# Three groups of token tiles in place of four, on a transformer block with a gathered expert layer

## The chip, the cores and the metric

The kernel runs on one core of a Trainium2 chip. The metric is device time in microseconds. Three runs of the kernel before gave 3733.66, 3748.12 and 3753.72; the median is 3748.12.

## What is computed

One trunk layer over 1024 latent tokens (8 tiles of 128) and 256 context tokens, width 1024, all in fp32. Cut to what matters:

```python
z = modulate(h_lat, sh_a, sc_a) @ w_in            # context tokens alike
q, k, v = mla_project(...)                         # 8 heads, 128 + 64 wide, low rank
att = softmax(q @ k.T * scale) @ v                 # keys: context and latent, 1280
s5 = bidirectional state-space layer               # second branch
merged = sigmoid(gate_mla) * att + sigmoid(gate_s5) * glu(s5)
h = layer_norm(ALPHA * h + g_a * (merged @ w_out), ln1)
# PEER: 8 heads, top 16 of 128 x 128 experts each
s = einsum(xb @ wq, keys); sv, si = top_k(s, 16)   # two halves
top_s, experts = top_k(sums of both halves, 16)    # 128 experts a token
act = gelu(einsum('thkd,td->thk', u_tab[experts], xb))
f = einsum('thk,thkd->td', softmax(top_s) * act, v_tab[experts])
out = layer_norm(ALPHA * h + g_f * f, ln2)
```

## The kernel before, in words

The 8 latent tiles are numbered 0 to 7. Up to about 480 us the input projection, the state-space layer, keys and values are made for all tiles and parked in HBM. Then the tiles go through in groups (`GROUPS`), here (0), (1, 2), (3, 4, 5), (6, 7). `front` does one group: `attention` (for each head the keys are loaded and split into a high and a low part once, then used for every tile of the group; a tile with a head is called a tile-head below), `gates` (weights of the gates and the GLU, loaded and split once a group), `close` (output projection and two norms), and the preparation of the next group's queries (`prepare`). It returns `route`, the expert selection of the group, which isn't run at once: the next group's `attention` takes `TSTEP` steps of it after each head. A step is one routing head.

The expert layer has three forms. Tiles 2 to 5 (`DENSE`) go through all 16384 experts as matmuls at the end (`dense`); after their routing, `spread` writes their weights as a matrix beside the next group's gates. Tiles 6 and 7 (`VEC`) gather rows of both tables beside the dense part. Tiles 0 and 1 gather too, in the front: for each of 128 experts a token, POOL issues an indirect DMA of a row of `peer_u` per token (L1271), DVE multiplies and sums it (L1275); then it gathers the row of `peer_v` (L1351) and PE adds it into two accumulators in PSUM by four matmuls with a diagonal (L1356). Six row buffers are shared by all gathers. The gathers of `peer_v` of a tile need all its 128 products; those of tile 0 lie between the gathers of tile 1.

The order on each engine is made by a scheduler from the written order, priorities (`PRIO`) and its own estimate of times; each engine then runs its instructions strictly in that order. `HOLDS` adds to this: a product of L1275 is placed behind a named instruction. For tile 0 the products from the 36th on stand behind the preparation of group 2 (mark p2), for tile 1 from the 100th on behind that of group 3 (p3). The dense part needs the two PSUM accumulators of tile 1's sum, so its second half of each step comes behind that sum.

Of the kernel before, what the change touches and what calls it, by code (L numbers as in the profile page):

```python
# [8 lines left out]
F32 = mybir.dt.float32  # L9
# [21 lines left out]
WBUFS = 4  # L31
NRES = 4
NEI = 3
RB = 6
SCB = (3, 3, 2, 2)
SC2 = (1, 1, 1, 1)
CAB = (1, 1, 1, 1)
OHB = (1, 1, 1, 1)
QHB = (2, 2, 1, 1)
H2B = 1  # L40
HMB = 2
GROUPS = ((0,), (1, 2), (3, 4, 5), (6, 7))
DENSE = (2, 3, 4, 5)
VEC = (6, 7)
TSTEP = (2, 2, 2)
TPRE = (0, 0, 0)
CHUNK = 32
GTP = 2
GTB = 2
VCUT = 2  # L50
STB = (1, 1, 1, 1)
SPLIT = (False, False, True, False)
SUBS = (((0,),), ((0, 1),), ((0, 1, 2),), ((0, 1),))
CENG = "VVVV"
WQB = 2
GSTEP = 10
# [2 lines left out]
RPRIO = 2500  # L59
MSTEP = 2  # L60
XLOAD = 4
GSIDE = ('right', 'right', 'right', None)
CSIDE = ("right", "right", "right", None)
SETTLE = 2
PREP = (0, 9, 9, None)
GSPLIT = (True, True, True, True)
GWB = 2
EBS = (2, 2, 2, 4)
EBANK = "S"
PRIO = (0, 1500, 1500, 3000, 2000)  # L70
PACE = 8
RAT = 3
TWAIT = 2
S0 = 36
P0 = 128
S1 = 100
P1 = 128
M0 = "p2"
M1 = "p3"
HOLDS = {0: [(M0, S0)] + [("r1.%d" % h, S0 + P0 * (h + 1)) for h in range(8)],  # L80
         1: [(M1, S1)] + [("r2.%d" % h, S1 + P1 * (h + 1)) for h in range(8)],
         6: [("t3", 0)]}
KENG = ((), (), (), ())
GENG = ((), (), (), ())
EVERY = (1, 2, 1)
LEAD = (0, 32, 0)

# [2 lines left out]
def block_kernel(ctx: ExitStack, tc: tile.TileContext, a: dict, out: bass.AP):  # L90
# [3 lines left out]
    def pool(name, bufs=1, side=None, space=None):  # L94
        kw = {"name": name, "bufs": bufs}
        if side:
            kw["side"] = side
        if space is not None:
            kw["space"] = space
        return tc.alloc_tile_pool(**kw)  # L100
# [24 lines left out]
    hm_d = tc.dram_tile([NT, 128, 8 * 128], F32, name="hm_d")  # L125
# [74 lines left out]
    W = pool("W")  # L200
# [3 lines left out]
    def wload(src, shape):  # L204

        t = W.tile([128, 2048], F32, tag="w", bufs=WBUFS, name="w")
        n = 1
        for d in shape[1:]:
            n *= d
        names = "abcd"[:len(shape) - 1]  # L210
        dims = {names[i]: shape[i + 1] for i in range(len(names))}
        flat = " ".join(names)
        v = t[:, 0:n] if len(shape) == 2 else t[:, 0:n].rearrange(f"p ({flat}) -> p {flat}", **dims)
        last[0] = SY.dma_start(v, src)
        return v
# [227 lines left out]
    for i in range(5):  # L443
        w = 1 << i
# [7 lines left out]
    t1, t2 = c32("sq0"), c32("sq1")  # L452
# [293 lines left out]
    def prepare_loads(gi):  # L746

        grp = GROUPS[gi]
        P = pool("P%d" % gi) if gi else None
        SY.dma_start(R["q"][2], a["rope_feat"][:, :, 128 * grp[0]:128 * grp[0] + 128 * len(grp)])  # L750
        if not gi:
            w = wload(a["w_cq"][0:2].rearrange("j p a b -> p j a b"), [128, 2, 8, 128])
            w = [w[:, 0], w[:, 1], wload(a["w_cq"][2], [128, 8, 128])]
            return P, w, [wload(hm_d[grp[0] + 2].rearrange("p (a b) -> p a b", a=8), [128, 8, 128])]
        w = P.tile([128, 3, 8, 128], F32, tag="wcq", name="wcq")
        hms = [P.tile([128, 8, 128], F32, tag="hm%d" % i, name="hm") for i in range(len(grp))]
        for i, l in enumerate(grp):
            SY.dma_start(hms[i], hm_d[l + 2].rearrange("p (a b) -> p a b", a=8))
            if i == 0:
                SY.dma_start(w, a["w_cq"].rearrange("j p a b -> p j a b"))  # L760
        return P, [w[:, j] for j in range(3)], hms

    def prepare(gi, P, w, hms):

        cqT = R["q"][1]
        for i, hmT in enumerate(hms):
            pa = bank("mm", "pa")
            for j in range(3):
                for k in range(8):
                    PE.matmul(pa[:, j * 128:(j + 1) * 128], hmT[:, k, :], w[j][:, k, :], start=(k == 0), stop=(k == 7))  # L770
            nq = (P or W).tile([128, 384 if P else 2048], F32, tag="nq" if P else "w", bufs=2 if P else WBUFS, name="nq")[:, 0:384]
            ss = cols.tile([128, 1], F32, tag="ss", name="ss")
            S.activation(nq, pa[:, 0:384], func=AF.Square, accum_out=ss)
            rs = rstd_of(ss, EPS, 1.0 / 384)
            marks["p%d" % gi] = V.tensor_scalar(nq, pa[:, 0:384], rs, None, op0=MUL)
            pt = bank("tp", "ptc", (128, 4, 128))
            for j in range(3):
                PE.transpose(pt[:, j, :], nq[:, j * 128:(j + 1) * 128], eye)
            for j in range(3):
                S.activation(cqT[:, j, i * 128:(i + 1) * 128], pt[:, j, :], func=AF.Copy, scale=qng[:, j:j + 1])  # L780
        if P:
            P.release()

    def open_queries(gi):
        Q = pool("Q%d" % gi, side="right")
# [201 lines left out]
    def route(gi, grp, H, h2T):  # L987
# [57 lines left out]
        places = []  # L1045
        for sub in SUBS[gi]:
            for h in range(8):
# [8 lines left out]
                for z in range(2):  # L1056
# [14 lines left out]
                    pz = bank("mm", "pz")  # L1071
                    sc_ = B.tile([128, ntok], F32, tag="sc", bufs=SCB[gi], name="sc")
                    for i in sub:
# [521 lines left out]
```

## Time and profile before

| | |
|---|---|
| median of 3 runs | 3748.12 us |
| profiled execution | 3734.93 us |
| its span, first to last instruction | 3733.2 us |
| mean granted TensorE clock | 0.948 |
| busy share PE, DVE, ACT, POOL | 90%, 79%, 35%, 40% |

Shares are of the whole span. PE's matmuls are pipelined and their ends are modelled, so a busy PE is not PE at its peak. Line numbers are those of the kernel before.

### The profile page before, as it was taken

How to read it: one execution, taken by the hardware profiler on the slowest of the kernel's cores; microseconds unless marked ns; L12 is line 12 of the kernel's file. 1: busy time of each engine (PE TensorE's matmuls, PEld its weight loads, DVE VectorE, ACT ScalarE, POOL GpSimd, SP SyncE). 2: the span in 40 equal slices, each digit the busy share in tenths (PEclk: the TensorE clock that was granted, in tenths of full speed). 3: DMA queues.
4: the chain of work that ended last, by engine and by line, in shares of the span. 5: the costliest groups of instructions: out<-in, count | busy, mean ns of one | idle time of the engine just before them, and what ended most of it. 6: DMA issues, size and time to landing. Idle time of an engine off the chain costs nothing.

```text
span 3733.2 us, 54383 instructions
## 1 busy us (share of the span) xinstructions
PE 3359.1 (90%) x20022; PEld 2733.2 (73%) x20022; DVE 2956.9 (79%) x6996; ACT 1297.7 (35%) x2329; POOL 1491.9 (40%) x1254
## 2 busy tenths in 40 slices
PE   5978888979779989869999969999999999999997
PEld 3745577869667668757769758878888888888885
DVE  7358755685798879689968877888888888889895
ACT  2223353443123444033345443333333333333332
POOL 5045400041355564443442100265655555546540
PEclk7978999989889989979999979999999999999998
DMA  8742276476698898987898763599999999989992
GB/s 280 236 85 73 89 264 228 156 301 244 224 347 309 316 338 324 362 308 289 295 355 314 296 232 124 181 368 340 330 342 333 339 335 340 340 325 355 340 328 79
DMA packets 348714, 1032.46 MB, mean 277 GB/s; under 512 B 46592, under 2 KB 142080, under 8 KB 322592
## 3 DMA queue, kind: packets, MB, share of 16 engines
q0 software_dynamic: 147456, 536.94, 39.3%
q1 hardware_dynamic: 164032, 462.20, 34.9%
q10 hardware_dynamic: 36960, 29.86, 2.5%
q8 instruction: 157, 2.57, 0.3%
q14 instruction: 109, 0.89, 0.1%
HBM read 961.27 MB, written 67.62 MB: 276 GB/s over the span
## 4 chain that ended last, share of the span: by engine, by line
PE 56%; DVE 9%; issue 8%; DMA 7%; ACT 2%; POOL 2%; DVEq 0%; POOLq 0%; ACTq 0%
PE turn L1235 6%; PE turn L1237 6%; PE turn L1236 6%; PE fd L1196 5%; PE fd L1197 5%; PE fd L1198 5%; DMA vb<-in_peer_v,eiT 4%; DVE ub L1275 3%; PE po L954 2%; PE acc L1356 2%; PE pqr L1066 2%; PE pe L1153 2%; DMA ub<-in_peer_u,ei 2%; POOL ub L1271 1%; PE po L809 1%
## 5 line engine op out<-in xcount | busy, mean ns | idle before, releaser
L1271 POOL DMA_INDIRECT ub<-in_peer_u,ei x512 | 654.9, 1279 | 1212.9 <-DVE ub L1275 438.4
L1275 DVE SCALAR_TENSOR_TENSOR ub<-ub,h 128x1024 f32<-128x1024 f32 x512 | 616.3, 1217 | 59.5 <-DMA ub<-in_peer_u,ei 59.2
L1318 POOL DMA_INDIRECT vb<-in_peer_v,ei x256 | 361.8, 1413 | 268.2 <-DVE f L1321 205.5
L1351 POOL DMA_INDIRECT vb<-in_peer_v,eiT x256 | 288.7, 1128 | 400.4 <-PE acc L1356 324.8
L1235 PE MATMUL turn<-hh,u 128*128 128x512 f32 x1024 | 401.7, 392 | 0.0
L1236 PE MATMUL turn<-hh,u 128*128 128x512 f32 x1024 | 400.2, 391 | 0.0
L1237 PE MATMUL turn<-hl,u 128*128 128x512 f32 x1024 | 400.1, 391 | 0.0
L1197 PE MATMUL fd<-v,kpe_l 128*128 128x512 f32 x887 | 351.7, 397 | 1.5 <-DVE kpe_l L234 1.5
L1198 PE MATMUL fd<-v,kpe_h 128*128 128x512 f32 x887 | 349.6, 394 | 0.0
L1196 PE MATMUL fd<-v,kpe_h 128*128 128x512 f32 x887 | 339.3, 396 | 0.0
L1321 DVE SCALAR_TENSOR_TENSOR f<-vb,zz,f 128x1024 f32<-128x1024 f32 x254 | 325.4, 1281 | 2.8 <-DMA vb<-in_peer_v,ei 0.2
L1239 ACT ACTIVATE act<-turn 128x512 f32<-128x512 f32 x128 | 76.6, 598 | 578.7 <-PE turn L1237 578.6
L233 ACT CAST v<-w 128x1024 fp32r<-128x1024 f32 x128 | 134.7, 1053 | 269.1 <-PE fd L1197 269.0
L1235 PEld LDWEIGHTS turn<-hh,u 128*128 128x128 f32 x1024 | 192.3, 188 | 42.0
L1237 PEld LDWEIGHTS turn<-hl,u 128*128 128x128 f32 x1024 | 192.3, 188 | 41.9
L1236 PEld LDWEIGHTS turn<-hh,u 128*128 128x128 f32 x1024 | 192.3, 188 | 40.4
L1356 PE MATMUL acc<-vb,diag 128*32 128x256 f32 x2048 | 159.8, 397 | 51.1 <-DMA vb<-in_peer_v,eiT 51.0
L1198 PEld LDWEIGHTS fd<-v,kpe_h 128*128 128x128 f32 x887 | 166.8, 188 | 41.4
L1196 PEld LDWEIGHTS fd<-v,kpe_h 128*128 128x128 f32 x887 | 166.9, 188 | 40.8
L1197 PEld LDWEIGHTS fd<-v,kpe_l 128*128 128x128 f32 x887 | 166.9, 188 | 40.5 <-DVE kpe_l L234 1.8
L234 DVE TENSOR_TENSOR v<-w,v 128x1024 fp32r<-128x1024 f32 x128 | 156.2, 1221 | 33.4 <-ACT v L233 32.8
L1241 DVE TENSOR_TENSOR act<-act,gt 128x512 f32<-128x512 f32 x128 | 88.6, 692 | 118.2 <-ACT act L1239 117.9
(421 smaller groups left out, 8143.2 us busy)
## 6 DMA issues: line engine op xcount, KB each, us to landing
w<-in_peer_uT SPq DMA_DIRECT2D x64, 1024.0 KB
w<-in_peer_v SPq DMA_DIRECT2D x64, 1024.0 KB
w<-in_peer_wq SPq DMA_DIRECT2D x32, 1024.0 KB
gT_d<-stage SPq DMA_DIRECT2D x16, 2048.0 KB
gt<-gT_d SPq DMA_DIRECT2D x32, 1024.0 KB
vh<-v_d SPq DMA_DIRECT2D x32, 640.0 KB
w<-k_d SPq DMA_DIRECT2D x32, 640.0 KB
w<-in_w_mod_b SPq DMA_DIRECT2D x16, 1024.0 KB
```

Source lines behind the costliest of these rows:

```text
L1196: PE.matmul(o, ah[:, ts], vh[:, cs], start=first, stop=False)
L1197: PE.matmul(o, al[:, ts], vh[:, cs], start=False, stop=False)
L1198: return PE.matmul(o, ah[:, ts], vl[:, cs], start=False, stop=final)
L1235: PE.matmul(turn, uh[:, k, :], hh[:, k, :], start=(k == 0), stop=False)
L1236: PE.matmul(turn, ul[:, k, :], hh[:, k, :], start=False, stop=False)
L1237: PE.matmul(turn, uh[:, k, :], hl[:, k, :], start=False, stop=(k == 7))
L1271: GP.indirect_dma_start(out=ub, out_offset=None, in_=a["peer_u"], in_offset=bass.IndirectOffsetOnAxis(ap=ei[:, s:s + 1], axis=0))
L1275: V.scalar_tensor_tensor(ub, ub, 1.0, h2, op0=MUL, op1=MUL, accum_out=dots[:, s:s + 1])
L1318: GP.indirect_dma_start(out=vb, out_offset=None, in_=a["peer_v"], in_offset=bass.IndirectOffsetOnAxis(ap=ei[:, s:s + 1], axis=0))
L1321: V.scalar_tensor_tensor(f, vb, z[:, s:s + 1], f, op0=MUL, op1=ADD)
L1351: GP.indirect_dma_start(out=vb, out_offset=None, in_=a["peer_v"], in_offset=bass.IndirectOffsetOnAxis(ap=eiT[:, t:t + 1], axis=0))
L1356: PE.matmul(acc[d // 2][o:o + 32, 256 * (d % 2):256 * (d % 2) + 256], dg[:, q, jj, :], vb[:, d * 256:(d + 1) * 256], start=False, stop=Fal ...
```

## The change

The groups become (0, 1, 2), (3, 4, 5), (6, 7). Routing of the first group runs as two sub-groups: eight steps for tile 0, two idle steps, then eight steps for tiles 1 and 2 and again two idle ones, three steps after each head. The marks p2, p3 and the holds of tiles 0 and 1 go; that of tile 6 stays, under the new group number. Several per-group buffer counts change: the routing of the first group has two score buffers and one query buffer, where before groups (0) and (1, 2) had three and two. Preparation of the second group comes behind the closing of all tiles of the first; before, that of (1, 2) came behind the closing norm of tile 0.

```diff
-SCB = (3, 3, 2, 2)
+SCB = (2, 2, 2)
-QHB = (2, 2, 1, 1)
+QHB = (1, 1, 1)
-GROUPS = ((0,), (1, 2), (3, 4, 5), (6, 7))
+GROUPS = ((0, 1, 2), (3, 4, 5), (6, 7))
-TSTEP = (2, 2, 2)
+TSTEP = (3, 2)
-SPLIT = (False, False, True, False)
-SUBS = (((0,),), ((0, 1),), ((0, 1, 2),), ((0, 1),))
+SPLIT = (False, True, False)
+SUBS = (((0,), (1, 2)), ((0, 1, 2),), ((0, 1),))
-PREP = (0, 9, 9, None)
+PREP = (9, 9, None)
-EBS = (2, 2, 2, 4)
+EBS = (2, 2, 4)
-PRIO = (0, 1500, 1500, 3000, 2000)
+PRIO = (0, 1500, 3000, 2000)
-RAT = 3
+RAT = 2
-HOLDS = {0: [(M0, S0)] + [("r1.%d" % h, S0 + P0 * (h + 1)) for h in range(8)],
-         1: [(M1, S1)] + [("r2.%d" % h, S1 + P1 * (h + 1)) for h in range(8)],
-         6: [("t3", 0)]}
+HOLDS = {6: [("t2", 0)]}
...
     def prepare_loads(gi):
         grp = GROUPS[gi]
-        P = pool("P%d" % gi) if gi else None
+        P = pool("P%d" % gi)
...
-            return P, w, [wload(hm_d[grp[0] + 2].rearrange("p (a b) -> p a b", a=8), [128, 8, 128])]
+            two = wload(hm_d[2:4].rearrange("l p (a b) -> p l a b", a=8), [128, 2, 8, 128])
+            return P, w, [two[:, 0], two[:, 1], wload(hm_d[4].rearrange("p (a b) -> p a b", a=8), [128, 8, 128])]
```

The gathers stand in the same order on POOL in both kernels. Three places of the new order matter. Lines of the changed kernel are 8 lower than before in these places.

On PE the first group's attention begins with the preparation (pa, ptc) and the query projection (pq) of its tiles. Before:

```order
L770 MATMUL pa<-w 128x128 x24
L778 MATMUL ptc<-eye,nq 128x128 x3
L821 MATMUL pq<-cqT,w 128x128 x12
L858 MATMUL pS<-kh,qnh 128x512 x2
L858 MATMUL pS<-kh,qnh 128x256
```

and now:

```order
L763 MATMUL pa<-w 128x128 x48
L771 MATMUL ptc<-eye,nq 128x128 x3
L763 MATMUL pa<-w 128x128 x24
L771 MATMUL ptc<-eye,nq 128x128 x6
L813 MATMUL pq<-cqT,w 128x384 x12
L850 MATMUL pS<-kh,qnh 128x512 x2
L850 MATMUL pS<-kh,qnh 128x256
```

Three tiles are prepared before the first score, and the projection's matmuls are as many, but three times as wide. No routing matmul stands before the end of this attention.

On DVE the ids of tile 0 (ei) are followed by its first product with a gathered row (ub). Before, this lies in the attention of tiles 1 and 2, whose maxima and sums are mx, mb and smx:

```order
L1034 SCALAR_TENSOR_TENSOR ef<-pi 128x64
L863 TENSOR_REDUCE mx<-pS 128x1
L234 TENSOR_TENSOR kl<-w,kh 128x512
L1103 CAST ei<-ef 128x128
...
L800 RECIPROCAL smx<-smx 128x1
L1275 SCALAR_TENSOR_TENSOR ub,dots<-ub,h_17879 128x1024
L863 TENSOR_REDUCE mx<-pS 128x1 x2
```

Now it lies in the attention of tiles 3, 4 and 5, behind its twelfth tile-head:

```order
L1026 SCALAR_TENSOR_TENSOR ef<-pi 128x64
L1095 CAST ei<-ef 128x128
L1101 CAST eiT<-ptE 128x128
L1267 SCALAR_TENSOR_TENSOR ub,dots<-ub,h_17468 128x1024
L986 MAX V_8531<-sc 128x8 x2
L1267 SCALAR_TENSOR_TENSOR ub,dots<-ub,h_17468 128x1024
```

The first products moved by one group; and where maxima of the attention stood among them, top-16 steps of the routing of tiles 1 and 2 (V) stand now. Up to the last sum of this attention 131 products follow.

On PE, at the end of the front, the last matmuls of tile 1's sum (acc) come before the routing of tiles 6 and 7 (pqr) and the dense part (turn). Before:

```order
L1356 MATMUL acc<-vb,diag 32x256 x4
L1337 MATMUL acc<-none 128x512 x2
L1153 MATMUL pe<-first,second 128x128 x48
...
L1153 MATMUL pe<-first,second 128x128 x64
L192 MATMUL tp<-eye,xr 128x128 x8
L1066 MATMUL pqr<-h2T,w 128x128 x16
L1235 MATMUL turn<-hh,u 128x512
```

and now:

```order
L1145 MATMUL pe<-first,second 128x128 x4
L1348 MATMUL acc<-vb,diag 32x256 x8
L1329 MATMUL acc<-none 128x512 x2
L1058 MATMUL pqr<-h2T,w 128x128 x16
L1066 MATMUL pz<-keysT,qh 128x128 x2
```

The matmuls of the spreading (pe) and the transposes of the closing (tp), which stood behind the sum, stand before it.

## Rows read from the trace of the kernel before

**Rows 1.** The page, busy us, share of the span, instructions.
```profile
PE 3359.1 (90%) x20022; PEld 2733.2 (73%) x20022; DVE 2956.9 (79%) x6996; ACT 1297.7 (35%) x2329; POOL 1491.9 (40%) x1254
```
**Rows 2.** Busy time by stretch: length, busy by engine (instructions), clock, DMA share, GB/s.
```profile
480.00:569.00 89.00, 74.44 (x485) 66.85 (x485) 48.35 (x126) 53.45 (x132) 0.00 (x0) 0.90 0.72 266
569.00:653.00 84.00, 68.95 (x466) 62.90 (x466) 51.89 (x110) 27.50 (x40) 0.00 (x0) 0.96 0.67 244
...
851.00:975.00 124.00, 116.25 (x832) 111.31 (x832) 71.23 (x160) 27.28 (x34) 1.87 (x2) 0.96 0.57 204
975.00:1340.00 365.00, 306.04 (x2180) 244.54 (x2181) 320.41 (x1059) 127.44 (x333) 204.07 (x182) 0.93 0.88 320
1340.00:1624.00 284.00, 232.72 (x1747) 200.56 (x1750) 231.02 (x532) 77.75 (x91) 140.27 (x106) 0.90 0.89 336
1624.00:1924.00 300.00, 284.11 (x2203) 215.31 (x2200) 242.95 (x1077) 118.38 (x285) 133.26 (x130) 0.97 0.85 306
1924.00:2212.00 288.00, 242.58 (x1976) 207.45 (x1975) 241.07 (x645) 138.44 (x153) 58.85 (x53) 0.92 0.79 300
2212.00:3733.00 1521.00, 1489.03 (x6720) 1215.21 (x6720) 1288.60 (x2058) 496.73 (x692) 714.21 (x512) 0.99 0.83 299
```
**Rows 3.** Gathers of peer_u on POOL by stretch (length, busy, count).
```profile
851.00:975.00 124.00, 1.87 (x2) 0.96 0.57 204
975.00:1340.00 365.00, 145.36 (x129) 0.93 0.88 320
1340.00:1624.00 284.00, 87.50 (x70) 0.90 0.89 336
1624.00:1924.00 300.00, 14.94 (x15) 0.97 0.85 306
```
**Rows 4.** Gathers of peer_v for tiles 0 and 1 by stretch.
```profile
975.00:1340.00 365.00, 58.72 (x53) 0.93 0.88 320
1340.00:1624.00 284.00, 52.77 (x36) 0.90 0.89 336
1624.00:1924.00 300.00, 118.32 (x115) 0.97 0.85 306
1924.00:2212.00 288.00, 58.85 (x53) 0.92 0.79 300
```
**Rows 5.** The page, DMA queue of all 1024 gathers: packets, MB, share.
```profile
q0 software_dynamic: 147456, 536.94, 39.3%
```
**Rows 6.** Waits between 970 and 2200: us in total, times, longest.
```profile
DVE ub L1275 <- DMA ub<-in_peer_u,ei: 40.8, 32, 4.9
...
POOL vb L1351 <- PE acc L1356: 324.8, 110, 21.0
```
**Rows 7.** Softmax sums of tile 0, its first two, and three preparations: first and last start.
```profile
L800 DVE RECIPROCAL smx<-smx x8: 162/164/166, 498.5 to 561.4; 128x1 f32<-128x1 f32 x8
...
L800 DVE RECIPROCAL smx<-smx x2: 162/163/164, 498.5 to 505.6; 128x1 f32<-128x1 f32 x2
...
L775 DVE TENSOR_SCALAR nq<-pa,rs_y x3: 610/617/618, 963.4 to 979.6; 128x384 f32<-128x384 f32 x3
```
**Rows 8.** Query projection by form: count, busy us, mean ns.
```profile
L821 PE MATMUL pq<-cqT,w 128*128 128x384 f32 x96 | 37.7, 539 | 7.3 <-DVE rl L828 2.8 <-DVE qr L828 2.6 <-ACT cqT L780 1.8
...
L821 PE MATMUL pq<-cqT,w 128*128 128x128 f32 x96 | 16.2, 319 | 3.2 <-DVE qr L828 1.4 <-ACT att L810 0.9 <-ACT cqT L780 0.9
```
**Rows 9.** Attention of tiles 1, 2 up to the ids of tile 0, as rows 2.
```profile
653.00:765.00 112.00, 105.12 (x749) 95.64 (x748) 82.65 (x366) 49.81 (x148) 0.00 (x0) 1.00 0.44 146
```
**Rows 10.** Gathers of peer_v in the 100 us that have most.
```profile
1800.00:1900.00 100.00, 54.57 (x54) 1.00 0.91 328
```
**Rows 11.** Gathers of tiles 6, 7 beside the dense part, both tables.
```profile
2380.00:3620.00 1240.00, 352.42 (x256) 1.00 0.93 336
2380.00:3620.00 1240.00, 361.79 (x256) 1.00 0.93 336
```
**Rows 12.** The page, products on DVE: count, busy us, mean ns, idle before.
```profile
L1275 DVE SCALAR_TENSOR_TENSOR ub<-ub,h 128x1024 f32<-128x1024 f32 x512 | 616.3, 1217 | 59.5 <-DMA ub<-in_peer_u,ei 59.2
```

More of the change, by code (lines that the diff above doesn't have):

```diff
@@ L34 @@
 RB = 6
-SCB = (3, 3, 2, 2)
-SC2 = (1, 1, 1, 1)
-CAB = (1, 1, 1, 1)
-OHB = (1, 1, 1, 1)
-QHB = (2, 2, 1, 1)
+SCB = (2, 2, 2)
+SC2 = (1, 1, 1)
+CAB = (1, 1, 1)
+OHB = (1, 1, 1)
+QHB = (1, 1, 1)
 H2B = 1
 HMB = 2
-GROUPS = ((0,), (1, 2), (3, 4, 5), (6, 7))
+GROUPS = ((0, 1, 2), (3, 4, 5), (6, 7))
 DENSE = (2, 3, 4, 5)
 VEC = (6, 7)
-TSTEP = (2, 2, 2)
-TPRE = (0, 0, 0)
+TSTEP = (3, 2)
+TPRE = (0, 0)
 CHUNK = 32
@@ L50 @@
 VCUT = 2
-STB = (1, 1, 1, 1)
-SPLIT = (False, False, True, False)
-SUBS = (((0,),), ((0, 1),), ((0, 1, 2),), ((0, 1),))
+STB = (1, 1, 1)
+SPLIT = (False, True, False)
+SUBS = (((0,), (1, 2)), ((0, 1, 2),), ((0, 1),))
 CENG = "VVVV"
@@ L61 @@
 XLOAD = 4
-GSIDE = ('right', 'right', 'right', None)
-CSIDE = ("right", "right", "right", None)
+GSIDE = ('right', 'right', None)
+CSIDE = ("right", "right", None)
 SETTLE = 2
-PREP = (0, 9, 9, None)
-GSPLIT = (True, True, True, True)
+PREP = (9, 9, None)
+GSPLIT = (True, True, True)
 GWB = 2
-EBS = (2, 2, 2, 4)
+EBS = (2, 2, 4)
 EBANK = "S"
-PRIO = (0, 1500, 1500, 3000, 2000)
+PRIO = (0, 1500, 3000, 2000)
 PACE = 8
-RAT = 3
+RAT = 2
 TWAIT = 2
[L74 to L79, printed above, removed]
-HOLDS = {0: [(M0, S0)] + [("r1.%d" % h, S0 + P0 * (h + 1)) for h in range(8)],
-         1: [(M1, S1)] + [("r2.%d" % h, S1 + P1 * (h + 1)) for h in range(8)],
-         6: [("t3", 0)]}
-KENG = ((), (), (), ())
-GENG = ((), (), (), ())
+HOLDS = {6: [("t2", 0)]}
+KENG = ((), (), ())
+GENG = ((), (), ())
 EVERY = (1, 2, 1)
@@ L770, in prepare @@
                     PE.matmul(pa[:, j * 128:(j + 1) * 128], hmT[:, k, :], w[j][:, k, :], start=(k == 0), stop=(k == 7))
-            nq = (P or W).tile([128, 384 if P else 2048], F32, tag="nq" if P else "w", bufs=2 if P else WBUFS, name="nq")[:, 0:384]
+            nq = P.tile([128, 384], F32, tag="nq", bufs=2, name="nq")
             ss = cols.tile([128, 1], F32, tag="ss", name="ss")
@@ L780, in prepare @@
                 S.activation(cqT[:, j, i * 128:(i + 1) * 128], pt[:, j, :], func=AF.Copy, scale=qng[:, j:j + 1])
-        if P:
-            P.release()
+        P.release()
     def open_queries(gi):
```

## Prediction

> **What bounds the kernel now.** I read the page's busy shares first. PE stands at 90% and DVE at 79% [rows 1], but a share over the whole span mixes stages, so the second view is the busy time by stretch, cut where the stages of the four groups end [rows 2]. The reader is to see three kinds of stretch there. From 2212 to the end PE is busy 1489 of 1521 us: the dense experts and the routing of tiles 6 and 7, which the change leaves alone. From 480 to 975 the groups (0) and (1, 2) run, at a DMA share of 0.57 to 0.72. From 975 to 2212 the DMA share is 0.79 to 0.89 at 300 to 336 GB/s while DVE is busy 231 to 320 us of 284 to 365. That is where the gathers of tiles 0 and 1 run.
>
> The third view counts these gathers by stretch: 129 + 53 = 182 from 975 to 1340, 70 + 36 = 106, 15 + 115 = 130, and 53 [rows 3, 4], together 471 of the 512 that two tiles take. Each moves 536.94 MB / 1024 = 0.524 MB [rows 5]. The fourth view is who waits: POOL waits 324.8 us for the products that free row buffers, while DVE waits only 40.8 us for gathers [rows 6]. So rows land, then stand until DVE or PE comes to them, and DVE comes in its own order. From 975 on the pace is 182 gathers in 365 us, 0.499 a us.
>
> **The change part by part.** I go by stretches of the profiled execution (span 3733.2, time 3734.93; the median of the runs is 3748.12, 13.2 above).
>
> *Attention of tiles 0, 1, 2 alone.* Before, the eight softmax sums of tile 0 start from 498.5 to 561.4, 62.9 apart in all, and the two heads of a pair are 7.1 apart [rows 7]. So the three gaps between pairs are (62.9 - 4 x 7.1) / 3 = 11.5 each. With three tiles a pair of heads has six sums: 4 x 5 x 7.1 = 142. The gaps between pairs grow by the wider query projection, 24 records a pair at 539 in place of 319 ns [rows 8], 5.3 us: 3 x 16.8 = 50. That is 192, or 129 more than now. Two more tiles are prepared ahead, 8.1 us each by the spacing of three in a row, 963.4 to 979.6 [rows 7]: 16. Their hm loads go through the ring of four weight buffers, which they fill with w_cq, so the first query weights wait on SP's queue for a buffer of that preparation; that lies inside the 16. The attention then ends at 569 + 145 = 714. Bounds: all 23 gaps at 7.1 give 29 less, all at 62.9 / 7 = 9.0 give 14 more.
>
> *Gates, closing, next preparation.* 84 us for one tile and 124 for two [rows 2], so 164 for three (150 to 184; the 284 that three tiles take later holds 106 gathers and is no measure). The next attention starts at 878 where it now starts at 975: 97 us won. In it lie the weights and keys that are loaded and split once less; their loads fall where the DMA share was 0.57 to 0.72, so I give them nothing of their own. That the next group is prepared behind all tiles and no longer behind the first costs nothing beyond this: the 124 has that order already.
>
> *Attention of tiles 3, 4, 5.* Routing of tile 0 now lies here, and the ids of tile 0 come after twelve of its 24 tile-heads (the second order piece). From 653 to 765 nine tile-heads and all routing of tile 0 took 112 us, with PE busy 105 and no gather [rows 9]. Three tile-heads more at 8 us, between the 7.1 and 9.0 above, give 136. So the first gather starts near 1014, now 765 [rows 9]. Behind it, up to the attention's last sum, the order has 131 products on DVE and 140 matmuls (four to a gather, 35) on PE: 166 gathers. At 0.499 a us that is 333. The best 100 us have 54 [rows 10]: 307. In the dense part 512 take 1240 us, 0.413 a us [rows 11]: 402. I take 333, the pace of the same stage. With 136 it makes 469, and the stretch ends at 1347, now 1340. So the 97 us are gone: PE and DVE had gathers beside the second group before, and now have none until 1014, and the same products must still follow.
>
> The hold is gone, but it now costs POOL a pause from 851 to 975 (two gathers) in which nothing of tile 0 is wanted; removing it wins nothing when the gathers start later than it ended. The routing of this group has fewer buffers (one query copy for two, two score copies for three). At worst each of its 32 steps waits 1 us: 0 to 32, and I take 0, since DVE is the later one there.
>
> *Gates and closing of 3, 4, 5.* 107 gathers in place of 106, same work: 284, to 1631.
>
> *Attention of 6, 7.* 53 products on DVE (20 stand there now) and 105 gathers on PE, 158 in place of 130. Routing is the same. The 33 more products on DVE cost 33 x 1.217 [rows 12] = 40. By the pace, 28 / 0.499 = 56; if PE alone set the stretch (284 of 300), 0. I take 40: 340, to 1971.
>
> *Gates and closing of 6, 7.* 81 gathers for 53. 81 / 0.499 = 162 fits into 288, DVE has no more to do than now (241 of 288): 288, to 2259, now 2212. Up to 56 more, since the last product of tile 1 now stands right ahead of the routing, where 116 matmuls of the spreading follow it now (third order piece).
>
> *The rest.* 1521 as now: 3780 span, 3782 as a time, 47 over 3734.93 or 1.3%. On the median that is 3748 + 47 = 3795.
>
> A second count, by bytes: 975 to 2212 moves 117 + 95 + 92 + 86 = 390 MB [rows 2], of it 471 x 0.524 = 247 gathered and 143 other. After the first gather the changed kernel has 268 + 135 = 403 MB to move. At 328 GB/s, the mean of the two busiest stretches, that takes 1229 us from 1014, to 2243, beside the 2259 above.
>
> The trace shows no stretch of [rows 2] above 336 GB/s. The Trainium skill, "DMA: Bandwidth & Descriptors" (Specifications), gives one core about 358 GB/s from HBM; an estimate by that page ends these bytes at 1014 + 1126 = 2140, where the gathers would no longer hold the front. By that rule the first rival below gains; the rows, at 300 to 336 with shares up to 0.89, speak for the slower end.
>
> **The rivals.**
>
> *Gathers don't set the pace* (faster). If PE and DVE work around them, the attention of 3, 4, 5 grows by one tile's routing alone, 112 - 9 x 7.1 = 48, to 413, and that of 6, 7 stays 300: 878 + 413 + 284 + 300 + 288 + 1521 + 2 = 3686, on the median 3699. For it: DVE waits only 40.8 us for gathers. Against it: the order puts 131 products on DVE into the later part of the stretch, where now the 129 gathers for such products spread over the whole of it. It decides if the gathers of that half run above 166 / 277 = 0.6 a us, which no row shows.
>
> *Nothing changes.* PE is the engine with the highest share, and it issues 48 matmuls less of 15,432. With the best pace, 0.54 a us, the middle stretch takes 443 and that of 6, 7 takes 316: 3732, on the median 3745. For it: 100 us at that pace exist. Against it: they lie where the granted clock is 1.00 and POOL gathers for PE alone. The Trainium skill, "Perfetto Trace Analysis" (Identifying the Most-Contended Engine), calls matmul busy time a poor measure, since matmuls are pipelined; from 975 to 1340 the trace agrees, weight loads busy 245 us and matmuls 306 of 365, and DVE 320.
>
> *The gathers crawl* (much slower). At the dense part's 0.413 a us the middle stretch takes 538 and that of 6, 7 takes 368: 3879, on the median 3892. For it: in that part too DVE and PE are full when a row lands. Against it: there the dense loads share the queues and PE sets the pace.
>
> *It doesn't do what it says:* tile 0 first in the routing, yet routing of tiles 1 and 2 already stands among its last steps in the DVE order, so the ids may come 20 us later; this is inside the range.
>
> **How the numbers follow.** Forecast 0.50, faster rival 0.12, no change 0.18, crawling 0.20. About 0.5% is what a measurement of this kernel can tell from no change: 3729 to 3767. So faster 0.12, same 0.18, slower 0.70. The range 3732 to 3868 leaves out the faster rival and the upper half of the crawling one, whose prices lie between 3795 and 3892.
>
> **What would show it.** Right: the attention of 3, 4, 5 starts near 880, the first gather issues near 1014 and not 765, some 166 gathers lie between there and 1350, the last matmul of tile 1's sum ends near 2245, right ahead of the dense part, and that starts near 2265 and runs as long as now. Wrong: an attention of 0, 1, 2 that is far from 192 us between its first and last sum; a pace above 0.55 or under 0.43 gathers a us behind 1014; or a dense part that starts before 2200, which would turn the sign.

## The result and the profile after

The changed kernel takes 3778.03 us (median of 5 runs, 3771.2 to 3782.11), the kernel before 3741.06 us on the same chip (5 runs, 3733.66 to 3753.72). The ratio is 1.0098, 95% interval [1.0078, 1.0118]: about 37 us slower. The forecast was 3795 us in a range of 3732 to 3868, and "slower" at 0.70. All differences in us below are differences of ratios times 3741; a difference of two ratios is good to about 10 us.

The profiled execution took 3776.99 us, span 3775.2, mean granted clock 0.943. The page's busy shares answer to [rows 1].

```profile
PE 3382.0 (90%) x19926; PEld 2725.0 (72%) x19926; DVE 2922.7 (77%) x6928; ACT 1262.3 (33%) x2275; POOL 1496.5 (40%) x1254
```

The shares say nothing of the loss, so the reader goes to the stretches. The columns are those of [rows 2]. Attention of (0, 1, 2), its gates, closing and next preparation, then attention of (3, 4, 5), its gates and closing, the same two of (6, 7), and the rest:

```profile
511.00:718.00 207.00, 186.54 (x1204) 160.52 (x1202) 87.74 (x224) 113.51 (x286) 0.00 (x0) 0.98 0.24 85
718.00:904.00 186.00, 175.18 (x1232) 163.29 (x1233) 99.43 (x244) 41.10 (x66) 0.00 (x0) 0.96 0.42 152
...
904.00:1356.00 452.00, 329.27 (x2243) 271.61 (x2241) 363.26 (x1299) 122.64 (x342) 193.95 (x169) 0.86 0.72 257
1356.00:1646.00 290.00, 246.93 (x1859) 210.60 (x1855) 245.27 (x557) 87.94 (x114) 156.40 (x120) 0.92 0.93 354
1646.00:1959.00 313.00, 275.64 (x1992) 206.27 (x1994) 268.27 (x1126) 109.86 (x266) 158.12 (x142) 0.93 0.86 312
1959.00:2256.00 297.00, 277.67 (x2345) 226.57 (x2337) 237.61 (x647) 144.37 (x164) 94.01 (x84) 0.97 0.88 335
2256.00:3775.00 1519.00, 1480.92 (x6653) 1205.17 (x6651) 1297.96 (x2061) 495.16 (x690) 708.30 (x512) 0.99 0.84 301
...
904.00:1040.00 136.00, 124.53 (x872) 110.40 (x871) 86.30 (x375) 58.12 (x168) 0.00 (x0) 0.99 0.34 116
1040.00:1356.00 316.00, 204.74 (x1374) 161.21 (x1372) 276.96 (x924) 64.52 (x174) 193.95 (x169) 0.81 0.88 318
```

The last two rows split the attention of (3, 4, 5) at the first gather. Ahead of it PE is busy 92% and DVE 63%; behind it DVE is busy 88%, PE 65%, and the granted clock falls to 0.81. In 200 us of it both show at their extremes, same view:

```profile
1115.00:1215.00 100.00, 58.86 (x412) 53.79 (x411) 94.28 (x309) 20.84 (x58) 64.37 (x53) 0.82 0.91 327
1215.00:1315.00 100.00, 48.35 (x244) 32.68 (x244) 93.72 (x332) 8.68 (x23) 64.69 (x54) 0.67 0.87 313
```

When each step came, from the view by lines (duration min/median/max in ns, then first and last start): softmax sums of (0, 1, 2), ids of tile 0, matmuls of the sums of tiles 0 and 1, dense part. They answer to [rows 7] and to the prediction's marks.

```profile
L792 DVE RECIPROCAL smx<-smx x24: 152/164/166, 518.7 to 704.7; 128x1 f32<-128x1 f32 x24
...
L1095 DVE CAST ei<-ef x1: 227/227/227, 1038.9 to 1038.9; 128x128 int32<-128x128 f32 x1
...
L1348 PE MATMUL acc<-vb,diag x2048: 379/379/637, 1297.8 to 2243.1; 128*32 128x256 f32 x187
...
L1227 PE MATMUL turn<-hh,u x1024: 387/389/500, 2255.8 to 3735.2; 128*128 128x512 f32 x171
```

The waits from 904 to 2250 answer to [rows 6]. POOL waits 605 us once for the ids, and 284.3 us for matmuls of the sums (324.8 before, where the window began at 970):

```profile
POOL ub L1263 <- DVE ei L1095: 605.3, 1, 605.3
POOL vb L1343 <- PE acc L1348: 284.3, 108, 21.4
...
POOL ub L1263 <- DVE ub L1267: 91.2, 44, 7.7
...
DVE ub L1267 <- DMA ub<-in_peer_u,ei: 34.7, 30, 4.7
```

To compare stages across kernels I cut every trace at the same marks: the first score matmul of a group, its last softmax sum, the first score matmul of the next, and for (6, 7) the first matmul of the dense part. Each cell below is a stage's length in us, with p, the products of tiles 0 and 1 that started in it, and a, the rows of `peer_v` summed in it (matmul records divided by 8; a few records can be missing). "From" is the first score matmul of (3, 4, 5). The last two columns are the dense part's start, and the time from it to the end.

```
              from | att. (3,4,5)  | gates (3,4,5) | att. (6,7)    | gates (6,7)  | dense rest
before         994 | 341 p122 a51  | 304 p 76 a39  | 273 p13 a100  | 305 p 0 a66  | 2218  1516
after          904 | 452 p131 a34  | 290 p 79 a39  | 313 p46 a94   | 297 p 0 a89  | 2256  1519
no experts
  before       979 | 257           | 240           | 236           | 263          | 1975  1522
  changed      893 | 304           | 239           | 236           | 261          | 1934  1520
late (before)  977 | 374 p148 a46  | 312 p 81 a41  | 285 p18 a99   | 311 p 0 a70  | 2259  1525
no hold (bef) 1038 | 299 p 48 a50  | 305 p 81 a41  | 278 p11 a102  | 310 p 0 a63  | 2231  1521
5 steps        903 | 471 p155 a45  | 310 p 80 a41  | 284 p21 a101  | 307 p 0 a69  | 2275  1523
one sub-group  898 | 379 p 92 a 0  | 320 p 74 a51  | 366 p90 a86   | 330 p 0 a97  | 2293  1532
hold           901 | 453 p131 a34  | 274 p 49 a24  | 356 p76 a90   | 331 p 0 a100 | 2315  1523
buffers        901 | 435 p131 a33  | 297 p 79 a40  | 312 p46 a99   | 305 p 0 a84  | 2249  1521
short products
  before       983 | 287 p104 a43  | 273 p 70 a35  | 268 p37 a80   | 321 p 0 a97  | 2131  1521
  changed      897 | 321 p 90 a 0  | 275 p 61 a44  | 263 p84 a42   | 331 p21 a70  | 2087  1646
half peer_v
  before      1003 | 357 p134 a58  | 288 p 64 a32  | 302 p13 a166  | 270 p 0 a 0  | 2219  1524
  changed      905 | 469 p151 a44  | 334 p105 a70  | 299 p 0 a142  | 264 p 0 a 0  | 2270  1523
```

After against before: the start 90 earlier, then +111, -14, +40, -8, and +3 in the rest: 42, the difference of the two spans. Each row is a single execution (that of late lies 10 us above the median of its runs, that of before 6 below), so a few us between two cells mean nothing.

### The profile page after: what moved, and what is told of

The parts are those of the page before. It is cut to its first block, busy times and chain, and to the rows that moved or that the text cites. A ratio compares the mean times of both kernels' runs of the same rounds, so it can differ in the third digit from the quotient of the medians.

```text
span 3775.2 us, 53927 instructions
## 1 busy us (share of the span) xinstructions
PE 3382.0 (90%) x19926; PEld 2725.0 (72%) x19926; DVE 2922.7 (77%) x6928; ACT 1262.3 (33%) x2275; POOL 1496.5 (40%) x1254
## 4 chain that ended last, share of the span: by engine, by line
PE 68%; DVE 17%; DMA 8%; issue 3%; ACT 2%; POOL 1%; ACTq 0%; SPq 0%; DVEq 0%; POOLq 0%
PE turn L1227 6%; PE turn L1229 6%; PE turn L1228 6%; PE fd L1189 5%; PE fd L1188 5%; PE fd L1190 5%; DVE ub L1267 4%; DMA ub<-in_peer_u,ei 3%; DMA vb<-in_peer_v,eiT 3%; PE po L801 2%; PE pe L1145 2%; PE acc L1348 2%; PE pqr L1058 2%; PE po L946 2%; PE pq L813 2%
## 5 line engine op out<-in xcount | busy, mean ns | idle before, releaser
L1263 POOL DMA_INDIRECT ub<-in_peer_u,ei x512 | 666.2, 1301 | 1279.8 <-DVE ei L1095 799.2
L1343 POOL DMA_INDIRECT vb<-in_peer_v,eiT x256 | 288.2, 1126 | 361.2 <-PE acc L1348 284.3
L1348 PE MATMUL acc<-vb,diag 128*32 128x256 f32 x2048 | 172.9, 412 | 46.0 <-DMA vb<-in_peer_v,eiT 44.5
```

The costliest lines, as they stand in the source:

```text
L1263: GP.indirect_dma_start(out=ub, out_offset=None, in_=a["peer_u"], in_offset=bass.IndirectOffsetOnAxis(ap=ei[:, s:s + 1], axis=0))
L1343: GP.indirect_dma_start(out=vb, out_offset=None, in_=a["peer_v"], in_offset=bass.IndirectOffsetOnAxis(ap=eiT[:, t:t + 1], axis=0))
L1348: PE.matmul(acc[d // 2][o:o + 32, 256 * (d % 2):256 * (d % 2) + 256], dg[:, q, jj, :], vb[:, d * 256:(d + 1) * 256], start=False, stop=Fal ...
```

## The experiments

**Without the expert layer of tiles 0 and 1.** What does the change do to the front when nothing is gathered there? The same edit in both kernels.

```diff
-            for _ in retrieve([l for l in range(NL) if l not in DENSE + VEC]):
-                pass
+            for l in (0, 1):
+                SY.dma_start(out[l], h1_d[l])
```

> The changed kernel without the expert layer of tiles 0 and 1 (their 512 gathers, the products and sums; their output is a copy of h1). Theory (late gathers): the merge of the groups wins 70 us by the start of the second attention, and only the gathers, which start 274 us later and run at about 0.5 a us, take it back; so without them this kernel is 40 to 80 us faster than the kernel before without them. Rival (the merged front is itself no faster, by its buffers or its order): both the same within 15 us, or this one slower.

> The kernel before without the expert layer of tiles 0 and 1 (as the other). Both theories: 200 to 330 us under the kernel before, since 256 products of 1.217 us leave DVE; only the distance to the changed kernel without them tells the theories apart.

Measured: 3458.12 us for the changed kernel, ratio to before 0.9244 [0.9228, 0.9259], and 3499.62 us for the kernel before, 0.9349 [0.9331, 0.9367]. Without gathers the change is a gain of 39 us. The gathers cost the changed kernel 319 us and the kernel before 244: the loss is made among them. By the spans the gathers cost the changed kernel 85 us more (321 against 236); the table puts 64 more into the attention of (3, 4, 5) (148 above the front without them, against 84) and 40 more into that of (6, 7) (77 against 37), and the rest together gives 19 back. The front alone grows by 47 us in the attention of (3, 4, 5) (304 against 257), which is tile 0's routing, and starts 86 earlier. The stretches of the changed kernel without experts, the first two being the attention of (3, 4, 5), cut 136 us after its start as above, and the third that of (6, 7):

```profile
893.00:1029.00 136.00, 124.71 (x873) 110.57 (x873) 86.30 (x375) 58.11 (x168) 0.00 (x0) 0.99 0.34 116
1029.00:1197.00 168.00, 154.33 (x1095) 137.01 (x1093) 130.46 (x651) 62.62 (x171) 0.00 (x0) 0.99 0.22 75
...
1437.00:1673.00 236.00, 203.92 (x1222) 183.90 (x1220) 203.80 (x991) 99.67 (x245) 0.00 (x0) 0.95 0.23 77
```

And the kernel before without experts, from the attention of (1, 2) to the end of that of (3, 4, 5):

```profile
653.00:979.00 326.00, 294.32 (x1999) 267.36 (x1998) 189.57 (x615) 123.06 (x289) 0.00 (x0) 0.95 0.45 159
979.00:1236.00 257.00, 243.07 (x1677) 214.76 (x1675) 167.26 (x757) 114.27 (x307) 0.00 (x0) 0.98 0.22 75
```

Here is the room that DVE has: 136 of 326 us idle beside the group (1, 2), and 90 of 257 in the attention of (3, 4, 5). In the changed kernel it has 38 of 168 idle behind the point where the ids come.

**Before without its holds, and after with more buffers.**

```diff
-HOLDS = {0: [(M0, S0)] + [("r1.%d" % h, S0 + P0 * (h + 1)) for h in range(8)],
-         1: [(M1, S1)] + [("r2.%d" % h, S1 + P1 * (h + 1)) for h in range(8)],
-         6: [("t3", 0)]}
+HOLDS = {6: [("t3", 0)]}
```

> The kernel before with four groups, and the holds of tiles 0 and 1 taken out. Theory (late gathers): the pause from 851 to 975 goes or shrinks, gathers are no later, so within 15 us of the kernel before. Rival (products that aren't held block DVE and are what costs): 25 to 45 us slower, as the changed kernel.

```diff
-SCB = (2, 2, 2)
-QHB = (1, 1, 1)
+SCB = (3, 2, 2)
+QHB = (2, 1, 1)
```

> The changed kernel with three score buffers and two query buffers for the routing of the first group, as the first groups of the kernel before have. PE waits 62 us in it for score copies (7 waits, up to 27 us). Rival (buffers): the loss goes, 25 to 45 us faster than the changed kernel, within 10 us of the kernel before. Theory (late gathers): those waits lie where the gathers set the pace, so at most 12 us faster than the changed kernel.

Measured: 3761.06 us, ratio 1.0062 [1.0042, 1.0081], without the holds: 23 us slower, between the two theories. More products lie ahead of the attention of (3, 4, 5) (p is 48 behind it, 122 before), it starts 44 later and runs 42 shorter; the three stages behind it lose 1, 5 and 5. With the buffers given back: 3774.0 us, 1.0095 [1.0077, 1.0113], in the whole no difference from the changed kernel. In the stages there is one: the attention of (3, 4, 5) takes 435 us instead of 452 with the same 131 products, and the two stages of gates give 15 of these 17 back (297 against 290, 305 against 297). Behind its first gather:

```profile
1034.00:1336.00 302.00, 198.62 (x1353) 155.63 (x1351) 277.98 (x925) 64.18 (x174) 197.94 (x168) 0.80 0.92 331
```

**Before with its products held back from the first one on.**

```diff
-S0 = 36
+S0 = 0
```

> The kernel before, with the products of tile 0 held from the first on (not from the 36th) behind the preparation of the third group, so that its gathers begin beside the attention of tiles 3, 4, 5, as in the changed kernel; groups, buffers and routing as before. Theory (late gathers): 36 products of 1.217 us, 44 us, move from a stretch with room into one without; the attention of tiles 1, 2 gets back up to 14 us: 20 to 60 us slower than the kernel before. Rival (the start of the gathers is not what costs): within 10 us of the kernel before.

Measured: 3776.2 us, ratio 1.0079 [1.0054, 1.0105], 30 us slower. The groups are those of before; only some products come later. DVE's products in the kernel before, from the attention of (1, 2) on (instructions are the products and their readouts):

```profile
994.00:1336.00 342.00, 149.76 (x246) 0.94 0.89 324
...
653.00:994.00 341.00, 52.73 (x89) 0.93 0.62 221
```

and with the hold from slot 0:

```profile
653.00:977.00 324.00, 10.64 (x18) 0.96 0.50 174
977.00:1351.00 374.00, 179.93 (x295) 0.90 0.90 326
```

42 us of products leave the first stretch and make it 17 shorter. 30 us of them enter the attention of (3, 4, 5) and make that 33 longer (374 against 341). The same product costs less than half of its time at the one place and all of it at the other. The stages behind add another 35 us in this execution, which is 51 longer than that of before, where the ratio of all runs gives 30.

**Earlier ids in the changed kernel.** Five routing steps after each head instead of three.

```diff
-TSTEP = (3, 2)
+TSTEP = (5, 2)
```

> The changed kernel with five routing steps of the first group after each head in place of three: the ids of tile 0 come after two to three heads and not four. Theory (late gathers): the first gather issues 30 to 60 us earlier, 15 to 30 gathers more lie ahead, and it is 10 to 40 us faster than the changed kernel. Rival (the gathers' start is not what costs, or the routing only moves PE's work): within 8 us of the changed kernel.

Measured: 3797.06 us, ratio 1.014 [1.0117, 1.0164], 16 us slower than the changed kernel, where I had expected 10 to 40 faster. The first gather came 37 us earlier, as meant:

```profile
L1263 POOL DMA_INDIRECT ub<-in_peer_u,ei x167: 932/1002/3064, 1003.0 to 1399.4; - x167
```

But the scheduler answered by placing 155 products in this attention instead of 131. It runs 471 us instead of 452, and the gates behind it 310 instead of 290; the attention of (6, 7) then saves 29 us, and its gates lose 10 again. The moved products are no loss by themselves: the two attentions together run 10 us shorter. The loss stands in the two stages of gates, which hold no more work of the gathers (80 products against 79, and 110 rows of the sums against 128). Their granted clock is lower, 0.87 against 0.92 and 0.92 against 0.97; whether that is cause or effect no run shows:

```profile
1374.00:1684.00 310.00, 251.97 (x1851) 213.76 (x1850) 246.32 (x560) 86.22 (x110) 155.72 (x122) 0.87 0.90 336
...
1968.00:2275.00 307.00, 257.39 (x2151) 219.82 (x2149) 241.65 (x649) 143.53 (x163) 73.86 (x65) 0.92 0.80 306
```

"The earlier the better" is wrong as a rule.

**Short products.** Products of tiles 0 and 1 over 128 of 1024 columns, in both kernels; transfers and matmuls stay.

```diff
-                V.scalar_tensor_tensor(ub, ub, 1.0, h2, op0=MUL, op1=MUL, accum_out=dots[:, s:s + 1])
+                c = slice(0, D if l in VEC else 128)
+                V.scalar_tensor_tensor(ub[:, c], ub[:, c], 1.0, h2[:, c], op0=MUL, op1=MUL, accum_out=dots[:, s:s + 1])
```

> The changed kernel with the products of tiles 0 and 1 over 128 of the 1024 columns (the rest of the sum is left out); all gathers move as before. Theory (DVE sets the pace of the gathers in the front): 256 products lose about 1 us each, and it is 150 to 250 us faster than the changed kernel. Rival (the transfers set the pace, at 330 GB/s and a DMA share of 0.9): at most 80 us faster, since 268 MB of gathered rows must pass all the same.

> The kernel before with the same short products for tiles 0 and 1. If DVE sets the pace: 130 to 230 us faster than the kernel before. If the transfers do: at most 80 us faster. The distance to the changed kernel with short products tells what the late start costs when DVE is relieved: late transfers would keep the changed kernel at least 30 us slower than this one, DVE's products alone would turn it 20 to 40 us faster, as without gathers.

Measured: 3739.62 us, ratio 1.0006 [0.999, 1.0022], for the changed kernel, and 3644.21 us, 0.9719 [0.9685, 0.9752], for the kernel before. The totals alone look as if the transfers held the changed kernel back, since it gains 34 us from DVE's relief and the other 105. The stages say more. In the changed kernel the attention of (3, 4, 5) falls from 452 to 321 us, 17 above the front without experts. Part of that is work that moved: 90 products and 96 gathers stand in it, and not 131 and 169. Behind the first gather the transfers run at 333 GB/s, with PE at 0.96 of its clock, and the gathers no faster than with full products, 96 in 184 us, 0.52 a us against 0.53:

```profile
897.00:1034.00 137.00, 125.82 (x884) 111.68 (x883) 86.45 (x375) 58.39 (x169) 1.10 (x1) 0.99 0.33 115
1034.00:1218.00 184.00, 158.79 (x1086) 138.07 (x1084) 146.86 (x832) 62.81 (x171) 93.01 (x96) 0.96 0.92 333
```

The run with one piece, below, has 92 full products and also 96 gathers in this stage, and takes 379 us. So at equal gathers the short products make it 58 us shorter, where DVE's time for them falls by 86 (112 us against 26).

The dense part starts at 2087, 169 earlier. Then the total loses most of that again: 70 + 42 + 44 = 156 of the 256 rows of the sums are done when it starts, the other matmuls run inside it (the last starts at 2282.2), and the rest takes 1646 instead of 1519. DVE's relief let the front go ahead of the gathers, whose pace did not rise:

```profile
L1349 PE MATMUL acc<-vb,diag x2048: 376/403/637, 1341.4 to 2282.2; 128*32 128x256 f32 x187
```

**Half the rows of peer_v.** Two slots share a row buffer, so 128 gathers (67 MB) go; products and matmuls stay.

```diff
-                        vb = rows.tile([128, D], F32, tag="row", name="vb")
-                        GP.indirect_dma_start(out=vb, out_offset=None, in_=a["peer_v"],
-                                              in_offset=bass.IndirectOffsetOnAxis(ap=eiT[:, t:t + 1], axis=0))
+                        if q % 2 == 0:
+                            vb = rows.tile([128, D], F32, tag="row", name="vb")
+                            GP.indirect_dma_start(out=vb, out_offset=None, in_=a["peer_v"],
+                                                  in_offset=bass.IndirectOffsetOnAxis(ap=eiT[:, t:t + 1], axis=0))
```

> The changed kernel with half of the rows of peer_v for tiles 0 and 1 fetched: two slots in a row share one row buffer, so 128 of the 512 gathers (67 MB) go away, while every product on DVE and every matmul stays; the sums are wrong by that. Theory, the transfers of the late gathers set the pace: from the first gather to the dense part it moves about 400 MB now, and 333 MB at the same 328 GB/s would end 200 us earlier; DVE, busy for 85% there, caps that. So 60 to 150 us faster than the changed kernel (3630 to 3720), more than the 38 us that the short products gave. Rival, DVE and PE set the pace with the products and matmuls themselves: all of these stay, so at most 30 us faster.

> The kernel before with the same half of the rows of peer_v for tiles 0 and 1 left out, all products and matmuls kept. Theory, the transfers have slack here because they begin 270 us earlier: 20 to 60 us faster than before (3680 to 3720), less than the changed kernel gains, so that the changed kernel's 37 us of loss shrink to nothing or turn. Rival, products and matmuls set the pace in both: at most 30 us faster in both, and the 37 us stay.

Measured: 3784.43 us, ratio 1.0069 [1.0047, 1.0091], for the changed kernel, 11 us less than with all rows and hardly to be told from it; 3739.86 us, 0.9948 [0.993, 0.9965], for the kernel before, 19 less. The theory that transfers set the pace falls; its rival expected at most 30 in both, and that the loss of the changed kernel stays. It stays: the ratios of the two differ by 0.0121, or 45 us. Gates of (3, 4, 5), then the stages of (6, 7), in the changed kernel:

```profile
1374.00:1708.00 334.00, 269.12 (x2091) 226.88 (x2092) 279.46 (x628) 89.15 (x115) 177.77 (x142) 0.87 0.93 346
1708.00:2006.00 298.00, 290.37 (x2371) 223.42 (x2371) 226.50 (x1041) 112.96 (x275) 71.57 (x67) 0.98 0.60 205
2006.00:2270.00 264.00, 216.25 (x1593) 205.42 (x1593) 233.17 (x625) 136.86 (x149) 0.00 (x0) 0.91 0.58 213
```

In the attention of (6, 7) the DMA share is 0.60 instead of 0.86, and it still takes 298 us: PE is busy 290 of them, and 142 rows of the sums stand there, 63 us above the 236 without experts, or 0.44 a row. No transfer is short there. The attention of (3, 4, 5) says the same: with five steps it holds 155 products and 204 gathers and takes 471 us, here 151 products and 176 gathers and 469. 28 gathers less, and 2 us. Behind the first gather, five steps and then this run:

```profile
1003.00:1374.00 371.00, 249.90 (x1719) 197.95 (x1717) 318.76 (x1010) 85.32 (x229) 238.03 (x204) 0.84 0.90 325
...
1041.00:1374.00 333.00, 215.08 (x1466) 171.77 (x1464) 299.79 (x963) 65.57 (x176) 205.46 (x176) 0.80 0.89 315
```

The edit also moved work, since the scheduler places products in earlier stages (151 and 105), so the whole time alone would not settle it.

**Routing of the first group in one piece, and a hold in the changed kernel.**

```diff
-TSTEP = (3, 2)
-SUBS = (((0,), (1, 2)), ((0, 1, 2),), ((0, 1),))
+TSTEP = (2, 2)
+SUBS = (((0, 1, 2),), ((0, 1, 2),), ((0, 1),))
```

> The changed kernel without one part of the change: the first group's routing takes tiles 0, 1 and 2 together in each of 8 steps instead of tile 0 alone first. By the order the ids of tile 0 come after 13 tile-heads of the second group (now 12) but behind the routing of all three tiles, two tiles of 48 us more: first gather near 1140 instead of 1040. Theory, a late start is what costs: 20 to 60 us slower than the changed kernel (3798 to 3838). Rival, the order inside the first group's routing is worth nothing, since the same products and routing follow in any order: within 10 us of 3778.

```diff
-HOLDS = {6: [("t2", 0)]}
+HOLDS = {1: [("p2", 40)], 6: [("t2", 0)]}
```

> The changed kernel with a hold of the kind that it gave up: the products of tile 1 from slot 40 on wait for the last preparation of the group (6, 7), so by the order 52 instead of 82 products lie in the gates and closing of (3, 4, 5), and 73 instead of 43 in the attention of (6, 7). Theory, the transfers set the pace and have no slack: a pause in the row buffers is lost, 10 to 50 us slower (3788 to 3828). Rival, products among the gates and the closing delay the front, as in the kernel before, where the holds are worth 20 us: 10 to 25 us faster (3753 to 3768).

Measured: 3826.11 us, ratio 1.0189 [1.016, 1.0217], with one piece, 34 us slower than the changed kernel; 3839.87 us, 1.0213 [1.0187, 1.0239], with the hold, 43 slower. Both lie where late gathers were expected to put them; that the hold's expectation names the transfers as the reason does not follow, after the runs above. With one piece the first gather starts at 1117, and 90 products land in the attention of (6, 7), which takes 366 us. From that gather to the end of the attention of (3, 4, 5), 96 gathers run, 0.60 a us, and DVE is busy 147 of 159 us:

```profile
1117.00:1276.00 159.00, 91.40 (x495) 75.67 (x495) 146.96 (x317) 47.15 (x122) 120.56 (x96) 0.79 0.93 329
```

With the hold, POOL issues 10 gathers in a stretch where DVE is idle for a third:

```profile
1515.00:1615.00 100.00, 80.25 (x492) 70.34 (x490) 64.75 (x185) 12.06 (x26) 12.70 (x10) 0.90 0.53 192
```

30 products move from the gates of (3, 4, 5), which win 16 us, to the attention of (6, 7), which loses 43; with 100 rows of the sums left for it, the last stage loses another 34.

## Why the prediction was right

**The start.** Predicted 97 us earlier, measured 90 on one mark (904 against 994). The attention of (0, 1, 2) took 186 us from first to last sum (predicted 192); from its last sum to the next group's first scores it is 199.4 us, where before the two tiles (1, 2) took 156.6 (+43, predicted +40 for the third tile).

**First gather.** Predicted 136 us behind the attention's start, measured 136 (904 to 1040). On the clock it is 26 later than the 1014 predicted: 19 because the mark 878 was the start of the last preparations and not of the first scores (975 against 994 before), 7 because 90 us were won and not 97.

**Attention of (3, 4, 5).** Predicted +104, measured +111, and 166 gathers against 169. The size held, and the reason given for it did not, so the close agreement is in part luck. I took the pace of the gathers, 0.499 a us, as what the stage obeys, and a count of bytes agreed. The runs show DVE instead: 28 gathers less at nearly the same products (151 and 155) saved 2 us, and short products at the same 96 gathers made it 58 us shorter. The front's own instructions keep DVE busy 130 us behind the first gather; the 131 products add 158.87 us. Together that is 289 us; the stage has DVE busy for 277 of 316, since neighbours overlap in part. In the five runs of the changed kernel with full products and tile 0 first in the routing the stage costs above its length without experts

```
           above 304   products   us a product
after         148        131         1.13
hold          149        131         1.14
5 steps       167        155         1.08
half peer_v   165        151         1.09
buffers       131        131         1.00
```

against 1.217 for the product itself [rows 12]. With two tiles' routing in the stage, in the kernel before, the same price is 84 / 122 = 0.69, and in its other runs with full products 0.75 (half `peer_v`), 0.79 (late) and 0.88 (no hold). The 45 products that ran ahead of 994 made the start 15 us later than without experts, 0.33 each; without the holds 116 of them made it 59 later, 0.51 each. That is where the gain went: the change takes away the cheap place and fills the dear one.

These prices put everything by which a stage grew down to its products. Rows of the sums are in them, and so may be a slower PE: without the sums it is busy 29 us longer in this stage than without experts (329.27 - 20.77 - 279.05), at a granted clock of 0.86 against 0.99. How much of the 148 us that is, no run shows. DVE's products, and then PE's matmuls of the sums in the first stage:

```profile
904.00:1356.00 452.00, 158.87 (x262) 0.86 0.72 257
1356.00:1646.00 290.00, 95.29 (x157) 0.92 0.93 354
1646.00:1959.00 313.00, 57.02 (x94) 0.93 0.86 312
...
904.00:1356.00 452.00, 20.77 (x272) 6.36 (x272) 0.86 0.72 257
```

That DVE sets the pace of the gathers too, since a row buffer comes free when its row is multiplied, is not shown: the short products did not raise it. In the chain of the profile from 1040 to 1356 the products have 25.8% and the landing of the gathers 24.6%:

```profile
by line: DVE ub L1267 25.8%; DMA ub<-in_peer_u,ei 20.6%; issue 8.4%; PE acc L1348 5.2%; DMA vb<-in_peer_v,eiT 4.0%; POOL ub L1263 3.9%; PE po L801 2.6%; DVE mx L855 2.3%; DVE I L990 2.2%; DVE I L987 2.0%; PE pq L813 1.9%; DVE sc L988 1.9%;
```

No run changed the number of row buffers, so what their round trip costs this stage stays open.

**Gates and closing of (3, 4, 5).** Predicted equal, measured 14 shorter, with 79 products against 76. I have no cause for the 14. In the runs with 74 to 81 full products in this stage its length goes with the granted clock: 290 us at 0.92, 297 at 0.90 (buffers), 304 and 305 at 0.89 (before, no hold), 312 at 0.88 (late), 310 at 0.87 (five steps), 320 at 0.85 (one piece). Which of the two follows from the other no run shows. Here the DMA share is 0.93 after the change, 0.92 with short products and 0.93 with half the rows of `peer_v`, so in this one stage the transfers are not ruled out as a limit. The prediction noted that no stretch passed 336 GB/s; this one moves 354, and 100 us of it move 382:

```profile
1504.00:1604.00 100.00, 91.92 (x643) 77.69 (x641) 72.67 (x169) 10.74 (x17) 48.97 (x43) 1.00 0.98 382
```

The Trainium skill, "DMA: Bandwidth & Descriptors" (Specifications), gives a core about 358 GB/s from HBM; this row lies above it, and the same page's section on bandwidth says that figure is the share with both cores of a pair streaming. So the prediction weighed a ceiling that does not bind in this row. The faster end that it gave did not come all the same: the 403 MB of the second count were 400, at 329 GB/s from 1040 to 2256, and with half the rows of `peer_v` the dense part started no sooner in either kernel (2270 and 2219).

**Attention of (6, 7).** Predicted +40, measured +40, by the step that it was given: 33 more products on DVE (46 against 13 on these marks, 53 against 20 in the prediction) at 1.217. DVE is busy 268 of 313 here, 86%, as it is without experts, 204 of 236.

**Gates of (6, 7) and the rest.** Predicted equal, measured 8 shorter and 3 longer. The last matmul of tile 1's sum starts at 2243.1, 13 us ahead of the dense part; the 56 us feared for it did not come. With five steps that sum ended at 2199 and the dense part started later all the same: the front, not the sum, decides there.

**Hold and buffers.** "Removing it wins nothing" stands for the changed kernel, where such a hold, on tile 1, costs 43. In the kernel before the holds are worth 23: without them the start comes 44 later, the next attention pays 42 of that back, and the rest stands in the later stages. That they pause the gathers while DVE still has idle time ahead is a guess. The buffers, which the prediction gave 0 of at most 32, are worth 17 us in the attention of (3, 4, 5) and nothing that the whole shows.

**The rivals.** "Gathers don't set the pace" had the growth of the front right (48, measured 47 without experts) and the sign wrong, since products come on top. "The gathers crawl" did not happen: 169 in the 316 us behind the first gather, 0.53 a us. "Nothing changes" missed the whole by 33 us as it was priced, but its 316 for the attention of (6, 7) doesn't follow from its own pace: 28 gathers more at 0.54 a us are 52 us, which makes 352 and 3781 on the median. So the total, 3778, would not tell that rival from the forecast; the stages do.

**Two readings that were wrong.** The 324.8 us of [rows 6] are POOL's waits for PE's matmuls of the sums and not for products. For the products it waited, in the same window before:

```profile
POOL ub L1271 <- DVE ub L1275: 212.1, 51, 124.4
```

After the change it is 91.2 against 284.3. That rows stand until DVE or PE comes to them holds either way. And PE issues 96 matmuls less, not 48 (20022 against 19926 on the pages).

The sum of 47 was 42 in the trace: no error above 14 us in a stage, and errors of both signs. Open stays what the value sums cost alone: no run took away PE's matmuls and kept the rest. The stages give 0.40 (36 us for 89 rows) to 0.71 us a row (69 for 97, one sub-group).

## What to carry to other kernels

Before moving background work to another stage, price it there by the engine that is full in that stage: the same product cost 0.33 to 0.51, 0.69 to 0.88 and 1.00 to 1.14 us at three places of this kernel. Fewer groups saved 39 us of front and still lost, since the work that had filled the gaps beside the old group (1, 2) had to go where one engine was already full. To find which resource sets a pace, relieve one at a time, in both kernels, compare stage by stage, and count the work in each stage, since a scheduler moves it: a shorter total can hide that the work has only moved behind the next mark, as it did with the short products.

## What the runs showed that I had not expected

- Full queues need not be the limit: a DMA share of 0.88 at 318 GB/s stood beside the attention of (3, 4, 5), and there 28 gathers less saved 2 us; with short products 0.92 at 333 GB/s stood beside a stage only 17 us above its length without gathers.
- PE's granted clock fell where PE stood idle half of the time beside a full DVE. Where DVE was busy 94 us of 100 and PE 48, the clock was 0.67, between its levels of 1.2 and 2.4 GHz; with the products cut short the same stage ran at 0.96.
- Opening the ids 37 us earlier made the whole 16 us slower. The scheduler moved 24 products forward, but the loss stands in the gates, at a lower granted clock, and its cause is open.
